# Last 16 units of attention as 8 units of two heads: plain fp32 P times V in two column halves, four products a visit, row sums by VectorE adds

## Chip, cores and metric

The kernel runs on one core of a Trainium2 chip. The metric is the device time of one execution in microseconds (us); lower is better. TensorE (PE, with its weight loads as PEld), VectorE (DVE), ScalarE (ACT), GpSimd (POOL) and SyncE (SP, which issues nearly all DMAs) run side by side, each in the order of its own queue, and wait for one another by semaphores.

## What is computed

Two layers of a diffusion backbone over 256 context and 2048 latent tokens of width 1024. Each layer projects the tokens (3100 columns), runs a bidirectional Mamba-2 scan (SSD), a bidirectional gated DeltaNet scan (GDN) and grouped-query attention (6 query heads, 2 key/value heads, head size 64) on the projections, and adds the gated and projected result to the stream. The part that the change touches:

```python
def block(qi):
    s = jnp.einsum('bqhgd,bkhd->bhgqk', qi, k).astype(jnp.float32) * scale
    pr = jax.nn.softmax(s, axis=-1).astype(v.dtype)
    return jnp.einsum('bhgqk,bkhd->bqhgd', pr, v)
```

Everything is float32, and the scores are large enough that the kernel subtracts each row's maximum before the exponential.

## The kernel before

Tokens stand in 18 tiles of 128 (`NT`). A layer goes through these stages: projections with the weights and tokens split into a high and a low fp32r part (L401, L455); `gating`, `gdn_pre` and `gdn_solve` of the GDN; `ssd_states` and `ssd_out` of the SSD, tile by tile; `gdn_chain`, a serial recurrence of 18 steps with two half-steps each; and the output projection (L1236). Attention is work that is laid beside all of these from the end of the projections on.

An attention unit is one head and 512 queries, 24 units a layer (the first layer has 6 small ones for the context beside them). `unit_max` makes the scores of the unit with queries as rows (`pq`, L536: four products of 512 columns and one of 256 for each of four query tiles), and DVE reduces them to row maxima (`mx`, L538). `unit_main` then goes over the 18 key tiles: two fp32r products give the scores with keys as rows and the maximum subtracted (`pst`, L567 and L568; together called S below), ACT writes exp of it (`pe`, L570), and `pv` (L561) multiplies by V, accumulating in the PSUM tile `po`. V carries a column of ones, so that row 64 of `po` is the row sum. The maxima of the next unit are spread over the key tiles of the present one.

For units 0 to 12 `pv` is one plain fp32 product, 65 columns wide. For units 13 to 23 ACT copies `pe` to fp32r (`ph`, L575), DVE takes the rest (`pl`, L576), V is split in the same way (`vh`, L659), and `pv` is three fp32r products. The exponentials stay in a ring of four tiles.

Order on the engines: the program is written with a priority by place in the text, and a scheduler lays the instructions of each engine in a fixed order. The text emits the first 8 attention units, then `gdn_chain`, then the other 16 units; so the chain goes ahead of units 8 to 23, and these fill what it leaves free. A half-step of the chain has three phases: products of the state on PE (`p<-Sc,kqc`, L1105 and L1114), DVE (`r`, L1109); products on PE (L1119), ACT (`Vc`, L1124); products on PE (L1128, L1130), DVE (new state `Sc`, L1132). `prep` loads the operands of a later step by DMAs on SP (`kqc`, `xf`, `acv`, `er`) into two buffers, and makes `pv` (L1072, L1081) from them.

## Time and profile before

| | us |
|---|---|
| median of 3 runs | 4045.18 (4043.82 to 4050.78) |
| the profiled execution, its own time | 4047.43 |
| its span, first to last instruction | 4045.6 |
| PE busy in it | 3760.3 (93%) |
| DVE busy | 2682.6 (66%) |
| ACT busy | 1831.1 (45%) |
| POOL busy | 1342.1 (33%) |

Busy is the union of an engine's instructions, so a PE instruction counts with the tail in which its last columns drain while the next one already streams. A window row gives the busy time of each engine in a stretch, the granted TensorE clock as a share of 2.4 GHz, and the DMA engines' share.

### The profile page before, as it was taken

Reading aid. Unit: us, or ns where it says so; the run is one execution under the profiler, and the core shown is the slowest. Engines: PE = TensorE matmul, PEld = TensorE weight load, DVE = VectorE, ACT = ScalarE, POOL = GpSimd, SP = SyncE. Lnnn points to the kernel's source line nnn. Section 1 sums busy time; section 2 is a strip of 40 time slices with the busy share of each in tenths; the row PEclk is TensorE's granted clock in tenths of the full one; section 3 lists DMA queues with packets and bytes.
Section 4 is the critical chain, followed back from the end, with each engine's and each line's share of the span. In section 5 each row is a group of like instructions: output and inputs, shape, how many; then the busy total and the mean of one; then the engine's idle time right before and its main releaser. Section 6 shows DMA issues by size and latency. Waiting matters only on the chain. (4 is left out here: it accounts for less than half of the span.)

```text
span 4045.6 us, 69921 instructions
## 1 busy us (share of the span) xinstructions
PE 3760.3 (93%) x25546; PEld 2839.3 (70%) x25546; DVE 2682.6 (66%) x5114; ACT 1831.1 (45%) x3782; POOL 1342.1 (33%) x1710
## 2 busy tenths in 40 slices
PE   8999999888999988887999999999889999889789
PEld 5899999554566655565678999995545566656567
DVE  7556473787778866665547664747886887666633
ACT  5343342443466655662224433424334566556510
POOL 5112130585267422233303130303762573112300
PEclk9999999999999989987999999999999999988889
DMA  6343432353312444547653434322443224444354
GB/s 201 100 141 111 133 110 92 107 156 136 103 55 64 90 108 107 127 100 235 206 168 112 152 104 136 112 99 79 145 135 105 58 66 96 104 103 114 91 173 153
DMA packets 554115, 484.38 MB, mean 120 GB/s; under 512 B 133992, under 2 KB 488620, under 8 KB 553772
## 3 DMA queue, kind: packets, MB, share of 16 engines
q1 hardware_dynamic: 511916, 444.51, 37.7%
q10 hardware_dynamic: 41856, 35.40, 2.9%
q8 instruction: 202, 3.31, 0.3%
q14 instruction: 141, 1.16, 0.1%
HBM read 335.59 MB, written 144.18 MB: 119 GB/s over the span
## 5 line engine op out<-in xcount | busy, mean ns | idle before, releaser
L570 ACT ACTIVATE pe<-pst 128x512 f32<-128x512 f32 (+1 forms) x876 | 512.0, 594 | 635.8 <-PE pst L568 602.2
L538 DVE TENSOR_REDUCE mx<-pq 128x1 f32<-128x512 f32 (+1 forms) x972 | 590.4, 626 | 134.8 <-PE pq L536 130.1
L561 PE MATMUL po<-pe,v 128*65 128x512 f32 x960 | 492.4, 602 | 3.9 <-ACT os__12072 L584 3.9
L536 PE MATMUL pq<-khh,q 128*128 128x512 f32 (+1 forms) x972 | 455.5, 499 | 29.8 <-DVE mx L538 25.9
L567 PE MATMUL pst<-q,khh 128*128 128x512 f32 (+1 forms) x876 | 437.5, 500 | 38.5 <-DVE mx L538 36.4
L455 PE MATMUL ps<-hi,wh 128*128 128x384 f32 (+2 forms) x1296 | 441.1, 340 | 0.0
L455 PE MATMUL ps<-lo,wh 128*128 128x384 f32 (+2 forms) x1296 | 441.1, 340 | 0.0
L455 PE MATMUL ps<-hi,wl 128*128 128x384 f32 (+2 forms) x1296 | 441.0, 340 | 0.0
L576 DVE TENSOR_TENSOR pl<-pe,ph 128x512 fp32r<-128x512 f32 x396 | 318.7, 809 | 108.7 <-ACT ph L575 68.9
L401 PE MATMUL ps<-wh,hi 128*128 128x320 f32 (+1 forms) x1120 | 354.4, 318 | 1.6 <-DVE hi L365 1.6
L568 PE MATMUL pst<-qm,klo 65*128 65x512 f32 (+1 forms) x876 | 355.1, 407 | 0.0
L401 PE MATMUL ps<-wh,lo 128*128 128x320 f32 (+1 forms) x1120 | 349.8, 315 | 1.7 <-DVE lo L366 1.7
L401 PE MATMUL ps<-wl,hi 128*128 128x320 f32 (+1 forms) x1120 | 350.4, 314 | 0.0
L536 PEld LDWEIGHTS pq<-khh,q 128*128 128x128 f32 x972 | 187.3, 195 | 185.0 <-issue 70.2
L376 DVE TENSOR_TENSOR wl<-wt,wh 128x1024 fp32r<-128x1024 f32 (+3 forms) x144 | 175.3, 1246 | 167.2 <-ACT wh L375 165.0
L567 PEld LDWEIGHTS pst<-q,khh 128*128 128x128 f32 x876 | 171.1, 195 | 156.8 <-DVE mx L538 64.1
L575 ACT CAST ph<-pe 128x512 fp32r<-128x512 f32 x396 | 243.5, 619 | 81.9 <-PE po L561 34.9
L561 PE MATMUL po<-ph,vh 128*65 128x512 f32 x792 | 270.1, 423 | 0.1
L455 PEld LDWEIGHTS ps<-lo,wh 128*128 128x128 f32 x1296 | 244.0, 188 | 10.3
L455 PEld LDWEIGHTS ps<-hi,wl 128*128 128x128 f32 x1296 | 243.4, 188 | 10.4
L455 PEld LDWEIGHTS ps<-hi,wh 128*128 128x128 f32 x1296 | 243.4, 188 | 10.2
L1236 PE MATMUL psd<-woh,mh 128*128 128x512 f32 x544 | 217.4, 400 | 16.4 <-ACT mh L1227 15.1
(587 smaller groups left out, 8086.9 us busy)
## 6 DMA issues: line engine op xcount, KB each, us to landing
wt<-in_w_in_dram SPq DMA_DIRECT2D x72, 512.0 KB
wmt<-in_w_mod_dram SPq DMA_DIRECT2D x48, 512.0 KB
pre_d<-pre SPq DMA_DIRECT2D x34, 512.0 KB
acv<-pre_d SPq DMA_DIRECT2D x34, 512.0 KB
kqc<-kt_d SPq DMA_DIRECT2D x68, 256.0 KB
acv<-pre_d SPq DMA_DIRECT2D x68, 256.0 KB
wt<-in_w_in_dram SPq DMA_DIRECT2D x24, 668.0 KB
wt<-in_w_in_dram SPq DMA_DIRECT2D x24, 640.0 KB
```

What stands on the lines that cost most here:

```text
L376: nc.vector.tensor_tensor(out=wl[:, ks, :], in0=wt, in1=wh[:, ks, :].bitcast(F32), op=ALU.subtract)
L401: nc.tensor.matmul(ps, hh[:, k, a], ww[:, k, :], start=(n == 0), stop=(n == 3 * KD - 1))
L455: nc.tensor.matmul(ps, ww[:, k, m * P:(m + 1) * P], hh[:, k, s0:s0 + sn], start=(n == 0), stop=(n == 3 * KD - 1))
L536: nc.tensor.matmul(pq[:, :n], q2[:, u * P:(u + 1) * P], khh[:, kvh, k0t * P + a:k0t * P + a + n], start=True, stop=True)
L538: nc.vector.tensor_reduce(mx[:, u, i:i + 1], pq[:, :n], axis=AX.X, op=ALU.max)
L561: nc.tensor.matmul(po[0:65, :qn], v[:, kt, vs], p[:, :qn], start=(kt == k0t and j == 0), stop=(kt == k1t - 1 and j == len(ops) - 1))
L567: nc.tensor.matmul(pt[:, :qn], khh[:, kvh, ks], q2[:, :qn], start=True, stop=False)
L568: nc.tensor.matmul(pt[:, :qn], klo[:, kvh, ks], qm[:, :qn], start=False, stop=True)
L570: nc.scalar.activation(out=pe[:, :qn], in_=pt[:, :qn], func=AF.Exp, scale=0.125)
L575: nc.scalar.copy(out=ph, in_=pe)
L576: nc.vector.tensor_tensor(out=pl, in0=pe, in1=ph.bitcast(F32), op=ALU.subtract)
L1236: nc.tensor.matmul(ps, a, w[k][:, n * 512:n * 512 + 512], start=(k == 0 and i == 0), stop=(k == KD - 1 and i == 2))
```

## The change

Units 0 to 7 stay as they are (plain fp32). Units 8 to 23 become eight pairs of neighbouring heads on the same queries. `pair_max` runs the two heads' maxima one after the other. `pair_main` makes for each key tile the scores and exponentials of both heads into one tile `pe` of 128 by 2 by 512. P times V is plain fp32, 64 columns of V without the ones: the first head's product writes partitions 0 to 63 of `po`, the second's 64 to 127. It is issued in visits of two key tiles, that is four products in the order head 0, head 1, head 0, head 1. The row sums no longer come from the column of ones: DVE adds the `pe` tiles into `acc` (one add of 128 by 1024 a key tile, 17 a pair), and at the pair's end two products by a matrix of ones sum `acc` over the partitions. The fp32r copies of P and V and their pool go. The ring of `pe` has six pair tiles in place of four single ones, the query rings four buffers in place of three.

```diff
+            def pair_main(h0, q0, qn, k0t, k1t, st):
+                kvh = (h0 // 3, (h0 + 1) // 3)
+                po = ps_o.tile([P, 512], F32, name="po", tag="po")
+                half = (slice(0, 64), slice(64, 128))
+                pend, acc = [], None
+
+                def visit(n, behind_mm):
+                    with tc.high_priority():
+                        for v in range(n):
+                            kt, pe = pend.pop(0)
+                            for j in range(2):
+                                c0 = kvh[j] * 65
+                                mm = nc.tensor.matmul(po[half[j]], v1[:, kt, c0:c0 + 64], pe[:, j], start=(kt == k0t), stop=(kt == k1t - 1))
+                                if v == 0 and j == 0:
+                                    behind(mm, behind_mm)
+
+                for kt in range(k0t, k1t):
+                    ks = slice(kt * P, (kt + 1) * P)
+                    pe = ap_.tile([P, 2, 512], F32, name="pe", bufs=PB)
+                    for j in range(2):
+                        pt = aslot("pst")
+                        nc.tensor.matmul(pt, khh[:, kvh[j], ks], st["q2"][j], start=True, stop=False)
+                        mm = nc.tensor.matmul(pt, klo[:, kvh[j], ks], st["qm"][j], start=False, stop=True)
+                        nc.scalar.activation(out=pe[:, j], in_=pt, func=AF.Exp, scale=0.125)
+                        if j == 0:
+                            yield
...
+                        nc.vector.tensor_tensor(out=acc, in0=acc, in1=pe, op=ALU.add)
+                    pend.append((kt, pe))
+                    if len(pend) == 3:
+                        visit(2, mm)
+                    yield
+                visit(len(pend), mm)
...
+                for j in range(2):
+                    nc.tensor.matmul(pl[half[j]], cc("ones")[:, 0:64], acc[:, j], start=True, stop=True)
...
-                    if kt in sp:
-                        ph = spl.tile([P, 512], F32R, name="ph", bufs=2)
-                        pl = spl.tile([P, 512], F32R, name="pl", bufs=2)
-                        nc.scalar.copy(out=ph, in_=pe)
-                        nc.vector.tensor_tensor(out=pl, in0=pe, in1=ph.bitcast(F32), op=ALU.subtract)
```

The order of the instructions moves in three places that matter below. Line numbers of the changed program are its own (two more up to the attention, 51 more in the chain).

First, SP at the end of the projections of the first layer. L526 and L527 load the queries of the first units; the others are projection weights (`wt`) and stores of its results. Before:

```order
L374 DMA wt<-in_w_in_dram 128x4x256
L188 DMA qkw<-in_q_norm_w_dram 128x64
L188 DMA qkw<-in_k_norm_w_dram 128x64
L335 DMA qt_d<-qo 128x128 x3
L526 DMA q_10914<-qt_d 128x512
L526 DMA q_10992<-qt_d 128x256
L526 DMA q_11026<-qt_d 128x512
L527 DMA qm<-qt_d 64x512
L527 DMA qm<-qt_d 64x256
L527 DMA qm<-qt_d 64x512
L488 DMA cv_d<-th 128x769
L374 DMA wt<-in_w_in_dram 128x4x256 x2
```

and in the changed program:

```order
L376 DMA wt<-in_w_in_dram 128x4x334 x2
L465 DMA zt_d<-z 128x384 x2
L411 DMA zn_d<-zn 128x334
L465 DMA zt_d<-z 128x384
L411 DMA zn_d<-zn 128x334 x5
L424 DMA zn_d<-zn 128x306 x5
L526 DMA q_10911<-qt_d 128x512
L526 DMA q_10989<-qt_d 128x256
L526 DMA q_11023<-qt_d 128x512
L526 DMA q_11207<-qt_d 128x256
L527 DMA qm<-qt_d 64x512
```

The loads moved from the middle of the last token group, with most of its weights still to be loaded, to behind nearly all its stores. On PE the 20 products of the first unit's maxima, which stood among the projection's, stand behind its last one. The second layer moves in the same way.

Second, DVE in `ssd_out`, about one token tile in its middle (`m`, `t`, `sq` are the SSD's, `mx` the attention's). Before:

```order
L844 TENSOR_TENSOR m_9978<-m_9978,pd 128x384
L862 TENSOR_TENSOR t_9893<-py,t_9893 128x384
L845 TENSOR_TENSOR m_9978<-m_9978,ee 128x384
L850 TENSOR_TENSOR t_9986<-po_10010,ecum 128x192
L850 TENSOR_TENSOR t_9987<-po_10010,ecum 128x192
L821 SCALAR_TENSOR_TENSOR m_10071<-cst,sp,m_10071 128x128 x6
L866 TENSOR_SCALAR sq<-sq 128x1
L850 TENSOR_TENSOR t_9986<-po_10035,ecum 128x192
L850 TENSOR_TENSOR t_9987<-po_10035,ecum 128x192
L868 TENSOR_SCALAR t_9893<-t_9893,sq 128x384
```

and in the changed program:

```order
L624 TENSOR_TENSOR acc<-acc,pe 128x1024
L538 TENSOR_REDUCE mx<-pq 128x1 x2
L913 TENSOR_TENSOR t_9890<-py,t_9890 128x384
L872 SCALAR_TENSOR_TENSOR m_10068<-cst,sp,m_10068 128x128 x6
L895 TENSOR_TENSOR m_9975<-m_9975,pd 128x384
L624 TENSOR_TENSOR acc<-acc,pe 128x1024
L896 TENSOR_TENSOR m_9975<-m_9975,ee 128x384
L917 TENSOR_SCALAR sq<-sq 128x1
L901 TENSOR_TENSOR t_9983<-po_10007,ecum 128x192
L901 TENSOR_TENSOR t_9984<-po_10007,ecum 128x192
L538 TENSOR_REDUCE mx<-pq 128x1 x2
```

Two to three adds stand in each tile, among the SSD's own instructions. From the first instruction of `ssd_out` to the chain's first, DVE has 105 `mx`, 39 `pl` and no add in the first layer before, and 111, none and 49 after; in the second layer 94, 31 and none, and 97, none and 43.

Third, PE in the middle of the chain of the first layer, from one half-step's first products (L1105, now L1156) to its last (L1128, now L1179). Before:

```order
L1105 MATMUL p<-Sc,kqc 64x64 x8
L1114 MATMUL p<-Sc,kqc 64x64 x2
L536 MATMUL pq<-khh,q_18401 128x256
L567 MATMUL pst<-q_18102,khh 128x512
L568 MATMUL pst<-qm,klo 128x512
L536 MATMUL pq<-khh,q_18401 128x512
L561 MATMUL po<-ph,vh_16904 65x512
L561 MATMUL po<-ph,vh_16905 65x512
L561 MATMUL po<-pl,vh_16904 65x512
L1119 MATMUL p<-r,xf_12683 64x64 x2
```

and in the changed program, with the phase that follows:

```order
L1156 MATMUL p<-Sc,kqc 64x64 x8
L1165 MATMUL p<-Sc,kqc 64x64 x2
L536 MATMUL pq<-khh,q_17927 128x512 x2
L613 MATMUL pst<-q_17702,khh 128x512
L614 MATMUL pst<-qm,klo 128x512
L1170 MATMUL p<-r,xf_12752 64x64 x2
...
L536 MATMUL pq<-khh,q_17927 128x256
L613 MATMUL pst<-q_17702,khh 128x512
L614 MATMUL pst<-qm,klo 128x512
L604 MATMUL po<-pe,v_352 64x512 x4
L536 MATMUL pq<-khh,q_17927 128x512 x2
```

The three P times V products between two phases are gone; a visit of four stands in about every third gap. In the whole chain PE has 158 S, 155 `pq` and 481 fp32r `pv` products in the first layer before, and 164, 137 and 42 visits after (second layer 167, 160 and 505; 169, 143 and 43). DVE has 159 `pl` before and 74 adds after (167 and 77). The last attention product stood two half-steps before the chain's end and stands four before it.

## Rows read from the trace of the kernel before

**Rows 1.** The page's first part: busy us, share of the span, instructions.

```profile
PE 3760.3 (93%) x25546; PEld 2839.3 (70%) x25546; DVE 2682.6 (66%) x5114; ACT 1831.1 (45%) x3782; POOL 1342.1 (33%) x1710
```

**Rows 2.** Windows of `ssd_out` and the chain, first and second layer.

```profile
core 0: us, PE busy (x) PEld busy (x) DVE busy (x) ACT busy (x) POOL busy (x), PEclk, DMA share, GB/s
1117.00:1393.00 276.00, 265.67 (x1251) 171.38 (x1249) 229.60 (x457) 189.79 (x492) 174.41 (x185) 1.00 0.25 66
1393.00:1836.00 443.00, 379.58 (x4994) 258.84 (x4994) 284.64 (x485) 256.78 (x494) 114.19 (x96) 0.89 0.50 116
3157.00:3393.00 236.00, 225.29 (x985) 144.22 (x984) 192.72 (x383) 150.97 (x395) 148.25 (x160) 0.97 0.22 59
3393.00:3836.00 443.00, 390.79 (x4986) 266.41 (x4984) 295.16 (x500) 267.76 (x515) 106.87 (x92) 0.91 0.47 107
```

**Rows 3.** Windows of `ssd_out` with plain units, then with split ones (columns as above).

```profile
1100.00:1296.00 196.00, 191.80 (x832) 120.05 (x830) 155.16 (x322) 124.56 (x339) 124.46 (x131) 1.00 0.20 59
1296.00:1392.00 96.00, 90.54 (x476) 60.33 (x475) 89.50 (x166) 71.31 (x166) 50.09 (x56) 0.99 0.31 72
...
3318.00:3380.00 62.00, 57.06 (x256) 38.23 (x255) 55.33 (x105) 40.80 (x99) 34.84 (x40) 0.94 0.19 49
```

**Rows 4.** Waits in the first layer's chain: who, for whom, us, times, longest.

```profile
POOL sd L1107 <- DVE Sc L1132: 187.6, 31, 8.6
...
DVE kqc L1061 <- DMA kqc<-kt_d: 42.0, 15, 4.2
...
DVE pl L576 <- ACT ph L575: 31.4, 43, 2.6
PEld pv L1072 <- issue: 24.7, 15, 4.3
...
DVE pl L576 <- PE po L561: 15.3, 18, 2.7
```

**Rows 5.** Timeline, PE around one tile of `ssd_states`: start, length, instructions.

```profile
1014.95 1.02 PE L561 MATMUL po<-pe,v 128*65 128x512 f32 x2
...
1015.90 0.87 PE L794 MATMUL pst<-xd,bn 128*64 128x192 f32 x8
1016.70 0.42 PEld L781 LDWEIGHTS pt<-cst,xb 128*128 128x128 f32 x4 [0.28 <-issue]
```

**Rows 6.** Timeline, PE in the chain: two fp32r products of P times V.

```profile
1608.09 0.63 PE L561 MATMUL po<-ph,vh 128*65 128x512 f32 x2
```

**Rows 7.** Groups by line and form: count, busy us, mean ns, idle before.

```profile
L576 DVE TENSOR_TENSOR pl<-pe,ph 128x512 fp32r<-128x512 f32 x396 | 318.7, 809 | 108.7 <-ACT ph L575 68.9 <-PE po L561 27.4 <-ACT vt L1076 5.0
L376 DVE TENSOR_TENSOR wl<-wt,wh 128x1024 fp32r<-128x1024 f32 x72 | 88.3, 1251 | 77.8 <-ACT wh L375 75.6 <-DMA q<-qt_d 2.2
L575 ACT CAST ph<-pe 128x512 fp32r<-128x512 f32 x396 | 243.5, 619 | 81.9 <-PE po L561 34.9 <-DVE pl L576 26.5 <-issue 2.8
```

**Rows 8.** Instructions of L576 in the chain: ns least, median, most.

```profile
L576 DVE TENSOR_TENSOR pl<-pe,ph x161: 673/692/1753, 1391.5 to 1812.9; 128x512 fp32r<-128x512 f32 x161
```

**Rows 9.** Groups of DVE in the first layer's `ssd_out`.

```profile
L538 DVE TENSOR_REDUCE mx<-pq 128x1 f32<-128x512 f32 x83 | 55.5, 678 | 14.8 <-PE pq L536 14.5
...
L576 DVE TENSOR_TENSOR pl<-pe,ph 128x512 fp32r<-128x512 f32 x38 | 32.7, 868 | 3.2 <-ACT ph L575 3.1
```

**Rows 10.** All maxima, from the page's fifth part.

```profile
L538 DVE TENSOR_REDUCE mx<-pq 128x1 f32<-128x512 f32 (+1 forms) x972 | 590.4, 626 | 134.8 <-PE pq L536 130.1
```

**Rows 11.** Timeline, the chain's last two states in the first layer.

```profile
1818.92 0.42 DVE L1132 TENSOR_TENSOR Sc<-sd,p 128x256 f32<-128x256 f32 x1
...
1825.24 0.36 DVE L1132 TENSOR_TENSOR Sc<-sd,p 128x256 f32<-128x256 f32 x1
```

**Rows 12.** The attention's start: a window behind the projections, and the split of V.

```profile
711.00:740.00 29.00, 25.21 (x91) 13.46 (x92) 25.51 (x49) 13.07 (x33) 4.96 (x8) 1.00 0.21 65
...
L659 DVE TENSOR_TENSOR vh<-v,vh 128x2322 fp32r<-128x2322 f32 x1 | 2.6, 2567 | 0.0
```

**Rows 13.** Groups of PE from 540 to 715 us: the first maxima among the projections.

```profile
L536 PE MATMUL pq<-khh,q 128*128 128x512 f32 (+1 forms) x24 | 8.6, 374 | 0.9 <-ACT pe L570 0.5 <-DVE mx L538 0.3
```

More of the change, by code (lines that the diff above doesn't have):

```diff
@@ L35 @@
 GT = 768
+PB = 6
+NS = 8
 def rev(t):
@@ L587, in unit_main, with pair_max @@
                 nc.sync.dma_start(mx_d[640 + h * 64:704 + h * 64, q0:q0 + qn], os_[ob:ob + 64, :qn])
+                yield
+            def pair_max(h0, q0, qn, k0t, k1t, st):
+                st.update(q2=[], qm=[])
+                gens = []
+                for j in range(2):
+                    sj = {}
+                    g = unit_max(h0 + j, q0, qn, k0t, k1t, sj)
+                    for i, _ in enumerate(g):
+                        if i == 0:
+                            st["q2"].append(sj["q2"])
+                            st["qm"].append(sj["qm"])
+                        yield
@@ new lines, in pair_main @@
+            def pair_main(h0, q0, qn, k0t, k1t, st):
[6 more added lines that the diff above has]
+                        for v in range(n):
+                            kt, pe = pend.pop(0)
+                            for j in range(2):
[12 more added lines that the diff above has]
+                        if j == 0:
+                            yield
+                    if kt == k0t:
+                        pass
+                    elif kt == k0t + 1:
+                        acc = ap_.tile([P, 2, 512], F32, name="acc", bufs=1)
+                        nc.vector.tensor_tensor(out=acc, in0=pend[0][1], in1=pe, op=ALU.add)
+                    else:
+                        nc.vector.tensor_tensor(out=acc, in0=acc, in1=pe, op=ALU.add)
+                    pend.append((kt, pe))
+                    if len(pend) == 3:
+                        visit(2, mm)
+                    yield
+                visit(len(pend), mm)
+                os_ = ap_.tile([P, 512], F32, name="os2", bufs=1)
+                nc.scalar.copy(out=os_, in_=po)
+                pl = aslot("pl")
+                for j in range(2):
+                    nc.tensor.matmul(pl[half[j]], cc("ones")[:, 0:64], acc[:, j], start=True, stop=True)
+                sm_ = ap_.tile([65, 512], F32, name="sm_", bufs=1)
+                nc.scalar.copy(out=sm_, in_=pl[0:65])
+                for j in range(2):
+                    nc.sync.dma_start(sm_d[None, HQ * q0 + (h0 + j) * qn:HQ * q0 + (h0 + j + 1) * qn], sm_[64 * j:64 * j + 1])
+                nc.sync.dma_start(mx_d[640 + h0 * 64:768 + h0 * 64, q0:q0 + qn], os_)
@@ L630, in attention @@
                 small = [] if last else [(h, 0, LC, 0, TC) for h in range(HQ)]
-                sb, ss_ = [{} for _ in big], [{} for _ in small]
-                mb = [unit_max(*un, st) for un, st in zip(big, sb)]
+                units = [(1, un) for un in big[:NS]] + [(2, un) for un in big[NS::2]]
+                sb, ss_ = [{} for _ in units], [{} for _ in small]
+                mb = [(unit_max if n == 1 else pair_max)(*un, st) for (n, un), st in zip(units, sb)]
                 ms = [unit_max(*un, st) for un, st in zip(small, ss_)]
@@ L653, in attention @@
                         pass
-                for i, un in enumerate(big):
-                    if i == 13:
-                        for _ in range(2):
-                            vh.append(spl.tile([P, NT, 129], F32R, name=f"vh{len(vh)}", bufs=1))
-                        nc.scalar.copy(out=vh[0], in_=v1)
-                        nc.vector.tensor_tensor(out=vh[1], in0=v1, in1=vh[0].bitcast(F32), op=ALU.subtract)
-                    spn = () if i < 13 else range(NT)
+                at = 0
+                for i, (n, un) in enumerate(units):
                     nxt = ms[i:i + 1] + mb[i + 1:i + 2]
-                    left = (21 + 3) * (i + 1 < len(big)) + 3 * (i < len(small))
+                    left = (24 * units[i + 1][0] if i + 1 < len(units) else 0) + 6 * (i < len(small))
+                    steps = n * (NT - 4)
                     done = 0
-                    for j, _ in enumerate(unit_main(*un, sb[i], spn)):
-                        want = left * (j + 1) // (NT - 4)
+                    for j, _ in enumerate((unit_main if n == 1 else pair_main)(*un, sb[i])):
+                        want = left * (j + 1) // steps
                         adv(nxt, want - done)
@@ L671, in attention @@
                             pass
-                    if i >= 14:
-                        next(side_work, None)
-                    if i % HQ == HQ - 1:
-                        if small and i == HQ - 1:
+                    at += n
+                    for k in range(at - n, at):
+                        if k >= 14:
+                            next(side_work, None)
+                    if at % HQ == 0:
+                        if small and at == HQ:
                             inv(0, LC)
-                        inv(big[i][1], 512)
+                        inv(un[1], 512)
                     yield
```

21 lines of the change are left out of this document (6 added, 15 removed).

## Prediction

> **What bounds the kernel now.** I read the page's first part, then windows stage by stage, then waits and single instructions in the stages that the change touches. Over the whole span PE is busy 93% and DVE 66% [rows 1], which would say that only PE's work counts. The windows say more [rows 2]: `ssd_out` takes 276 and 236 us with PE at 96 and 95%, the chain 443 us in both layers with PE at 86 and 88%, DVE at 64 and 67%, ACT at 58 and 60%, and a granted clock of 0.89 and 0.91.
>
> Inside `ssd_out` the bound depends on the attention beside it [rows 3]. With plain units PE is busy 191.80 of 196 us (98%) and DVE 79%; with split units DVE is busy 89.50 of 96 us (93%) and PE 94%; in the second layer's split stretch they are at 89 and 92%. So split units, which give DVE a subtraction a key tile, already bring it to the point where it limits. The chain is no engine's alone: 36 half-steps in 443 us are 12.3 us each, while the last two states, with no attention between them, stand 6.3 us apart [rows 11]. Attention roughly doubles a half-step. Waits there [rows 4]: GpSimd waits 187.6 us for the state, which is the recurrence; DVE 42.0 us for the load of `kqc`; and DVE 31.4 us for `ph` and 15.3 us for `po` ahead of `pl`, both waits that come from the split.
>
> **PE.** A plain product of 65x512 is two passes that together take 1.02 us [rows 5], and two fp32r products take 0.63 us [rows 6]. Both hold a tail that the next instruction overlaps. With a pass of 0.23 us for fp32r the tail is 0.63 − 2 × 0.23 = 0.17, three split products cost 0.69, and a plain one costs 1.02 − 0.17 = 0.85, or 0.43 a pass. The trace has no plain 512-column product on a half of the columns, but eight records of 192 columns on two halves: 0.87 us [rows 5]. A pass of 192 columns is 0.43 × 192/512 = 0.16 us; four overlapped steps and the tail make 0.81, eight in turn 1.45. So the halves run together. The changes of form cost something: from the plain product's start to L794's are 0.95 us instead of 0.85, and from there to the next line's 0.80 instead of 0.64. I allow 0.3 us a visit for both. A visit is then 4 × 0.43 + 0.3 = 2.0 us for four products, where four split products cost 2.76 and four plain ones 3.4. The bounds are 1.7 (no cost of the change) and 3.7 (no overlap).
>
> **DVE.** Out go the subtractions, 0.69 us at the median in the chain [rows 8] and 0.868 in `ssd_out` [rows 9]. In come adds of 128x1024, not in the trace. The nearest row is L376, 128x1024 with two inputs, 1.251 us [rows 7]. `pl` was 0.176 us longer beside the busy GpSimd of `ssd_out` than in the chain. One such wait an instruction would make an add 1.43 us there, and in proportion to its length it would be 1.25 × 0.868/0.692 = 1.57. I take 1.4, bounds 1.25 and 1.57. In the chain I take 1.25.
>
> The Trainium skill ("SBUF — State Buffer", section "SBUF: two separate sides") says that GpSimd and a VectorE operation with two SBUF inputs take a shared port as an exclusive lock for a whole instruction. The longer `pl` beside a busy GpSimd agrees. By the rule an add waits once as `pl` does (1.43 us), and it speaks against this change too, since longer instructions keep GpSimd out for longer; the sum by it would be 2 to 3 us higher.
>
> **`ssd_out`.** Between the same instructions the first layer gets 6 more maxima at 0.626 us [rows 10], 49 adds, and loses 39 `pl`: DVE 229.6 + 3.8 + 49 × 1.4 − 39 × 0.868 = 268.1 us. The second layer gets 3 maxima, 43 adds, and loses 31: 192.7 + 1.9 + 60.2 − 26.9 = 227.9. DVE alone then nearly fills the old length. At the 93% of the split stretch the stages become 288.3 and 245.0 us: **+21 us** in sum. PE doesn't contradict this, it has room at 94%. Bounds: at 97% busy and adds of 1.25 us, 269 and 228 us (−15); at 89% and 1.57 us, 311 and 264 us (+63). GpSimd, at 174 of 276 us, would at worst wait out the 35 us that the two-input work grows by (68.6 − 33.9), and stays at 76%.
>
> **Chain.** PE in the first layer: 481 products × 0.23 = 111 us go, 42 visits × 2.0 and 4 us of row sums come; 18 fewer `pq` save 4 and 6 more S of two products cost 3: −24 us. The second: 116 against 90, −4, +1: −29. DVE: 159 × 0.69 go, 74 × 1.25 come, 18 maxima go: −29, second layer −31. ACT loses 159 and 167 copies of 0.619 us [rows 7]: −98 and −103. No engine gets more. PE's −24 at a share of 86% is 28 us. The two more half-steps without attention at the end, at 6.3 us instead of 12.3, I count at little, since what stood there is done in fuller half-steps before. The 46.7 us in which DVE waited ahead of `pl` lose their cause, though how much of them ended a half-step can't be seen. Against that, the loads of `prep` pace a part (42.0 us of waits for `kqc`), and a visit of 2.0 us in one piece can stand ahead of a phase's products where three products of 0.23 us stood. I take −30 a layer, **−60 us**. Bounds: 0, if loads and the recurrence set the pace, and −75 a layer (28 + 46.7), if those waits all count.
>
> **Start of attention.** The first unit's maxima leave the projections: 20 × 0.23 = 4.6 us of PE less in a stage that PE bounds ([rows 13]: 24 instructions at 8.6 us with their tails). They now stand behind it and go at DVE's pace, 20 × 0.63 = 12.6 us, in a stretch that was nearly full, PE 25.21 and DVE 25.51 of 29 us [rows 12]. `vh`, 2.6 us of DVE, goes. Between −4.6, if gating covers all, and 12.6 − 2.6 = +10, if PE idles for all of it, I take +4 a layer, nearer the full price since both engines were nearly full: **+8 us**, bounds −9 and +20. The attention that this delays is in the counts of the later stages already.
>
> What I cost at nothing: row-sum products, 1.1 us eight times a layer, in the counts above for the chain and otherwise beside a DVE that limits; the larger ring of exponentials; ACT, which no window here shows over 75% busy.
>
> **Sum** against the profiled execution, 4047.4, which stands 2.2 us above the median of the runs: 4047.4 + 21 − 60 + 8 = 4016 us.
>
> **Rivals.**
>
> 1. DVE loses more in `ssd_out`, and the kernel ends slower. An add stands 1.4 us in DVE's queue ahead of the SSD's own instructions (`m`, `t`, `sq`), on which PE, GpSimd and ACT wait in turn; a `pl` stood 0.87. For it: two to three adds stand in each token tile, and 89 to 93% was reached with the shorter instruction. Against: two thirds of DVE's instructions there are no part of a tile's own sequence and can fill. With DVE at 85% the stages are 315 and 268 us, +71 and 4047 + 71 − 60 + 8 = 4066 us. It decides from a loss of 60 us, at 86.5% busy. Chance 0.20.
>
> 2. The chain is paced by its loads and waits, and gains nothing: 4076 us. For it: the DVE's wait for `kqc`, PE's share of only 86%, and half-steps of the same 443 us in both layers though PE's busy time differs by 11 us [rows 2]. Against: 6.3 us a half-step where no attention stands between. Chance 0.17.
>
> 3. The stalls of the split go with it, and the chain gains 75 us a layer: 3926 us. For it: DVE, ACT and PE all get less work, and nothing but attention makes a half-step 12 us. Against: the phases still wait in the order of the queues. Chance 0.13.
>
> 4. The halves don't run together with 512 columns, so that the change doesn't do what it says: 4 × 0.43 = 1.7 us more a visit, 85 visits in both chains, +145 us and some of the others on top: 4190 us. Against it stands the row of L794. Chance 0.04.
>
> The forecast keeps 0.46.
>
> **How the numbers follow.** No change can be told within 0.2%, 8 us: 4037 to 4053. The forecast's own range, 3975 to 4055, takes the terms' bounds at about half their reach; 0.38 of its chance lies below 4037 and 0.08 within. Rival 3 is faster throughout; rivals 1 and 2 spread 40 us around their times and give 0.05 to no change and 0.03 to faster; the rest and rival 4 are slower. Faster 0.54, same 0.13, slower 0.33. From 3940 to 4085 the range leaves out rival 4, most of rival 3 and the upper third of the first two, some 2 in 10.
>
> **What the profile after would show.** Products of a visit: the two halves' starts some ns apart, a visit of 2.0 us (1.7 to 3.7). Adds: a mean of 1.4 us in `ssd_out`, 1.25 in the chain. `ssd_out`: 288 and 245 us with DVE at 93% and PE well under 95%; PE at 96% again would show that DVE doesn't bound. The chain: about 413 us, half-steps of 11.4 us, DVE's wait for `kqc` still there; 443 us with that wait grown speaks for rival 2. Behind the projections: an idle PE of some us among the first maxima. A stage outside these that differs by more than 5 us (projections, `gdn_pre`, `gdn_solve`, output projection), or a lower clock in the chain because PE idles more, would make the sum wrong.

## The result and the profile after

The changed kernel takes 4214.91 us (median of 4 runs, 4193.2 to 4221.08) against 4047.98 us: a ratio of 1.0404, with an interval of 1.0364 to 1.0443. It is 4% slower, outside the range of 3940 to 4085 us and on the other side of the forecast 4016. Every ratio here and below is to runs of the kernel before that were made beside it (medians of 4033.70 to 4040.22 us for the experiments), so ratios can be compared with one another, and times only roughly.

The first two parts of its page, busy time of each engine and the granted clock of TensorE in 40 slices (9 is full), beside [rows 1]:

```profile
PE 3843.6 (91%) x25214; PEld 2769.7 (66%) x25214; DVE 2743.5 (65%) x4988; ACT 1601.7 (38%) x3384; POOL 1365.5 (32%) x1710
...
PEclk8999998999989977787999999999999788788889
```

PE's share of the span falls from 93 to 91% though its busy time grows by 83 us, and the mean granted clock falls from 0.959 to 0.913. DVE's busy time grows by 61 us of 4200 and stays at 65%: no engine's busy time shows where 171 us went. The windows do. `ssd_out` and the chain, first layer and second; `ssd_out` is taken from PE's first `py` product (L861, now L912) to its first product of the state (L1105, now L1156), and the chain from there to the last phase:

```profile
core 0: us, PE busy (x) PEld busy (x) DVE busy (x) ACT busy (x) POOL busy (x), PEclk, DMA share, GB/s
...
1138.00:1459.00 321.00, 285.88 (x1213) 166.01 (x1213) 263.90 (x452) 159.74 (x429) 183.49 (x181) 0.86 0.22 57
1459.00:1941.00 482.00, 407.98 (x4880) 234.52 (x4879) 278.50 (x391) 175.64 (x349) 127.62 (x101) 0.80 0.49 116
...
3266.00:3557.00 291.00, 263.94 (x1045) 153.91 (x1045) 227.09 (x399) 140.88 (x376) 154.70 (x157) 0.82 0.21 56
3557.00:4006.00 449.00, 390.98 (x4765) 225.02 (x4769) 263.59 (x384) 166.49 (x339) 105.44 (x91) 0.83 0.45 104
```

and the kernel before, cut in the same way:

```profile
1127.00:1396.00 269.00, 257.74 (x1215) 166.38 (x1214) 222.89 (x439) 180.61 (x465) 168.64 (x179) 0.99 0.27 69
1396.00:1824.00 428.00, 373.54 (x4972) 256.28 (x4974) 279.18 (x477) 252.69 (x488) 109.75 (x93) 0.90 0.48 112
...
3162.00:3400.00 238.00, 226.71 (x1052) 145.89 (x1051) 193.68 (x382) 153.41 (x399) 145.71 (x157) 0.97 0.25 64
3400.00:3832.00 432.00, 384.09 (x4902) 262.16 (x4903) 287.49 (x484) 261.41 (x504) 104.14 (x89) 0.91 0.46 106
```

So `ssd_out` grew by 52 and 53 us, the chain by 54 and 17, and the stretch ahead of `ssd_out`, in which the first pairs run, by 17 and 13; all other stages together gave 35 us back, 17 of them between the first layer's chain and the end of its output projection (267 us for 284). In `ssd_out` the clock went from 0.99 and 0.97 to 0.86 and 0.82, and PE is idle for 35 and 27 us, where it was idle for 11 in each. No engine is full: DVE is busy 82 and 78% (83 and 81% before), PE 89 and 91%. PE's waits for maxima in the first `ssd_out`, before and after (us, times, longest):

```profile
PE pst L567 <- DVE mx L538: 2.6, 5, 0.7
PE pq L536 <- DVE mx L538: 2.1, 6, 0.5
```
```profile
PE pq L536 <- DVE mx L538: 6.8, 9, 1.8
PE pst L613 <- DVE mx L538: 6.1, 6, 1.9
```

What PE did before its clock fell is seen at one place. Timeline of PE and DVE in `ssd_out`:

```profile
start us, us, engine line op out<-in xcount [idle before <-releaser]
...
1251.75 2.88 DVE L872 SCALAR_TENSOR_TENSOR m<-cst,sp,m 128x128 f32<-128x128 f32 x4
1251.97 0.59 PE L891 MATMUL pd<-rr,sufr 128*128 128x384 f32 x2 [1.10 <-DVE t L901]
...
1253.60 0.39 PE L614 MATMUL pst<-qm,klo 65*128 65x512 f32 x1
1254.56 1.01 DVE L538 TENSOR_REDUCE mx<-pq 128x1 f32<-128x512 f32 x2
1255.29 1.22 PE L536 MATMUL pq<-khh,q 128*128 128x512 f32 x2 [1.30 <-DVE mx L538]
```

and the windows around it:

```profile
1240.80:1247.60 6.80, 6.80 (x31) 3.95 (x28) 3.62 (x7) 1.37 (x4) 1.00 (x1) 0.72 0.07 19
1247.60:1254.90 7.30, 5.28 (x25) 3.59 (x24) 6.20 (x10) 4.95 (x16) 6.60 (x7) 1.00 0.19 54
1254.90:1261.70 6.80, 6.41 (x14) 2.98 (x16) 6.80 (x12) 1.58 (x4) 1.71 (x2) 0.50 0.17 48
1261.70:1268.50 6.80, 6.21 (x35) 4.31 (x31) 6.54 (x12) 2.68 (x6) 3.99 (x5) 1.00 0.02 4
```

PE waits twice for DVE, 1.10 us for `t` and 1.30 us for a maximum that stands in DVE's queue behind four instructions of the SSD. It is busy 5.28 of 7.30 us; then the granted clock is 0.50 for 6.8 us, and in that stretch PE gets through 14 instructions instead of 25 to 35. By an estimate, half of the 6.41 us in which PE was busy at half clock, the two waits of together 2.4 us cost some 3.2 us more. DVE is busy for all of the slow stretch. The place is not an exception: 76 stretches at half clock begin in this trace, and ahead of 75 of them, over a time as long as the second row, PE had idled for more than its 9% of the whole span (30% at the median).

For the whole kernel this can be added up from the page and the mean clock: PE's idle time is the span less its busy time, and the loss by the clock is taken as (1 − mean clock) × span, as if PE were busy in all of it.

| | ratio to before | span, us | PE busy, us | clock | idle, us | loss by clock, us | the rest, us |
|---|---|---|---|---|---|---|---|
| before | 1 | 4045.6 | 3760.3 | 0.959 | 285 | 166 | 3594 |
| after | 1.0404 | 4216.8 | 3843.6 | 0.913 | 373 | 367 | 3477 |
| no_adds | 1.0054 | 4078.1 | 3785.4 | 0.927 | 293 | 298 | 3488 |
| every_2nd | 1.0246 | 4135.2 | 3786.5 | 0.926 | 349 | 306 | 3481 |
| dup | 1.0426 | 4221.3 | 3900.6 | 0.935 | 321 | 274 | 3626 |
| no_adds_dup | 1.0258 | 4127.5 | 3847.2 | 0.948 | 280 | 215 | 3633 |
| nohp | 1.0416 | 4203.7 | 3926.8 | 0.956 | 277 | 185 | 3742 |
| same_half | 1.0728 | 4342.5 | 4038.9 | 0.930 | 304 | 304 | 3735 |
| ns24 | 1.0025 | 4038.5 | 3803.6 | 0.972 | 235 | 113 | 3691 |
| single64 | 1.0381 | 4190.2 | 4022.5 | 0.971 | 168 | 122 | 3901 |

The rest is, by this estimate, PE's work at full clock. The change cut it by 117 us, and got 88 us of idle time and 201 us of clock for it. The other rows belong to the experiments below.

### The profile page after: what moved, and what is told of

It reads as the page before. It is cut to its first block, busy times and chain, and to the rows that moved or that the text cites. A ratio compares the mean times of both kernels' runs of the same rounds, so it can differ in the third digit from the quotient of the medians.

```text
span 4216.8 us, 68181 instructions
## 1 busy us (share of the span) xinstructions
PE 3843.6 (91%) x25214; PEld 2769.7 (66%) x25214; DVE 2743.5 (65%) x4988; ACT 1601.7 (38%) x3384; POOL 1365.5 (32%) x1710
## 5 line engine op out<-in xcount | busy, mean ns | idle before, releaser
L615 ACT ACTIVATE pe<-pst 128x512 f32<-128x512 f32 x576 | 335.0, 595 | 577.7 <-PE pst L614 572.9
L624 DVE TENSOR_TENSOR acc<-acc,pe 128x1024 f32<-128x1024 f32 x256 | 349.6, 1366 | 94.1 <-ACT pe L615 92.3
L604 PE MATMUL po<-pe,v 128*64 128x512 f32 x1152 | 364.2, 732 | 0.0
L613 PE MATMUL pst<-q,khh 128*128 128x512 f32 x576 | 291.9, 507 | 26.4 <-DVE mx L538 14.6
L558 PE MATMUL po<-pe,v 128*65 128x512 f32 x600 | 304.4, 598 | 1.4 <-ACT os__11633 L574 0.9
L378 DVE TENSOR_TENSOR wl<-wt,wh 128x1024 fp32r<-128x1024 f32 (+3 forms) x144 | 175.2, 1247 | 176.0 <-ACT wh L377 175.9
L566 ACT ACTIVATE pe<-pst 128x512 f32<-128x512 f32 x300 | 172.8, 589 | 294.0 <-PE pst L564 292.3
L614 PE MATMUL pst<-qm,klo 65*128 65x512 f32 x576 | 255.5, 444 | 0.0
L1287 PE MATMUL psd<-woh,ml 128*128 128x512 f32 x544 | 215.9, 397 | 0.3
```

The source lines that it names most:

```text
L378: nc.vector.tensor_tensor(out=wl[:, ks, :], in0=wt, in1=wh[:, ks, :].bitcast(F32), op=ALU.subtract)
L558: nc.tensor.matmul(po[0:65, :qn], v1[:, kt, kvh * 64:kvh * 64 + 65], pe[:, :qn], start=(kt == k0t), stop=(kt == k1t - 1))
L604: mm = nc.tensor.matmul(po[half[j]], v1[:, kt, c0:c0 + 64], pe[:, j], start=(kt == k0t), stop=(kt == k1t - 1))
L613: nc.tensor.matmul(pt, khh[:, kvh[j], ks], st["q2"][j], start=True, stop=False)
L614: mm = nc.tensor.matmul(pt, klo[:, kvh[j], ks], st["qm"][j], start=False, stop=True)
L615: nc.scalar.activation(out=pe[:, j], in_=pt, func=AF.Exp, scale=0.125)
```

## Experiments

Theory A, formed from this: the adds hold up DVE, PE idles in short gaps, and the gaps halve its clock. Rivals: B, products on a column half bring the clock down by themselves; C, the order makes PE wait (visits of four products ahead of others, loads); D, PE's work sets the time.

**no_adds.** The adds go, and the row sums are made from a constant tile.

```diff
+            one_ = ap_.tile([P, 2, 512], F32, name="one_", bufs=1)
...
-                    if kt == k0t:
-                        pass
-                    elif kt == k0t + 1:
-                        acc = ap_.tile([P, 2, 512], F32, name="acc", bufs=1)
-                        nc.vector.tensor_tensor(out=acc, in0=pend[0][1], in1=pe, op=ALU.add)
-                    else:
-                        nc.vector.tensor_tensor(out=acc, in0=acc, in1=pe, op=ALU.add)
+                    acc = one_
```

> The changed kernel with the adds of the exponentials left out (the row sums are taken from a constant tile, so 136 VectorE adds a layer go and nothing else). Theory A, the adds hold up VectorE, TensorE then idles ahead of the maxima and its clock falls: the two ssd_out stages come back from 321 and 291 us to 265 to 280 and 235 to 250, TensorE's idle time there from 35 us to under 15, the clock there to 0.95 or more, and the time is 4040 to 4100 us. Theory B, the column halves themselves bring the clock down: it stays at 0.82 to 0.88 in both stages and the time stays above 4170. Theory C, the order (visits, loads) makes TensorE wait: the stages stay within 15 us of 321 and 291 and the time above 4150.

4051.34 us, 1.0054 (1.0031 to 1.0077). The adds cost 3.5% of the time, about 140 us. The profiled execution was the slowest of seven, 4079.9. Its windows:

```profile
1120.00:1432.00 312.00, 291.23 (x1222) 171.32 (x1222) 193.75 (x404) 159.75 (x429) 159.86 (x178) 0.86 0.23 60
1432.00:1865.00 433.00, 382.54 (x4878) 221.40 (x4878) 177.85 (x314) 173.82 (x351) 118.84 (x100) 0.85 0.53 126
3176.00:3433.00 257.00, 241.12 (x1085) 143.30 (x1083) 174.78 (x353) 142.69 (x382) 140.65 (x159) 0.91 0.23 63
3433.00:3867.00 434.00, 393.09 (x4757) 230.85 (x4755) 163.55 (x304) 164.74 (x338) 96.72 (x89) 0.83 0.45 106
```

The total is as theory A had it, its places only partly: the chain comes back to 433 and 434 us and the second `ssd_out` to 257, but the first stays at 312 at a clock of 0.86, with DVE busy 62%. So gaps and a low clock come without the adds too. GpSimd changes as well: in `ssd_out` it is busy 183.49 and 154.70 us with the adds and 159.86 and 140.65 without, for about as many instructions. How much of the price comes by way of this longer GpSimd, no run here separates.

**every_2nd.** Every second add is left out.

```diff
-                        nc.vector.tensor_tensor(out=acc, in0=pend[0][1], in1=pe, op=ALU.add)
-                    else:
+                        nc.vector.tensor_tensor(out=acc, in0=one_, in1=pe, op=ALU.add)
+                    elif kt % 2 == 0:
```

> Every second add left out (9 of 17 a pair stay; the row sums are wrong by it, and nothing else is left out). If the price follows VectorE's time: 1.020 to 1.028 of before, halfway. If one add in a row is hidden and only two close together delay the maxima and the chain: 1.003 to 1.015.

4137.64 us, 1.0246 (1.0225 to 1.0266): about halfway between 1.0404 and 1.0054, as the number of adds would have it. Its windows:

```profile
1130.00:1426.00 296.00, 270.35 (x1188) 161.98 (x1189) 224.57 (x421) 157.69 (x425) 173.61 (x180) 0.88 0.24 62
1426.00:1903.00 477.00, 403.82 (x4912) 228.82 (x4913) 234.44 (x363) 178.13 (x355) 123.70 (x101) 0.83 0.53 125
3218.00:3486.00 268.00, 242.28 (x1051) 143.93 (x1051) 199.32 (x374) 139.03 (x375) 150.82 (x159) 0.88 0.23 61
3486.00:3934.00 448.00, 383.65 (x4749) 221.96 (x4751) 221.86 (x352) 166.03 (x340) 106.07 (x93) 0.85 0.47 112
```

Stage by stage it is not halfway. Both `ssd_out` get back about half of their loss (296 and 268 us), but the chains, 477 and 448, stay within 5 us of the changed kernel's: there half of the adds cost as much as all, with DVE busy 49%. The first `ssd_out` is even shorter than the 312 us of no_adds, whose profile is of its slowest execution; a single stage of one profile is worth no more than that.

**half_adds** and **adds_late.** Each add as two of 128x512; or each add written with its visit, one to two key tiles later.

```diff
...
-                        nc.vector.tensor_tensor(out=acc, in0=acc, in1=pe, op=ALU.add)
+                    for j in range(2):
+                        if kt > k0t:
+                            a0 = (pend[0][1] if kt == k0t + 1 else acc)[:, j]
+                            nc.vector.tensor_tensor(out=acc[:, j], in0=a0, in1=pe[:, j], op=ALU.add)
```
```diff
                     if len(pend) == 3:
+                        add(pend[:2])
                         visit(2, mm)
...
```

> The changed kernel with each add of 128x1024 made as two of 128x512, the first behind the first head's exponential. The same elements; some 0.1 us more of VectorE a key tile for the second instruction. If the length in the queue is what delays the maxima (A1): TensorE's idle time in the ssd_out stages falls from 35 and 27 us by a third or more, time 4120 to 4170. If VectorE's total does it (A2): idle time and stages as before or longer, 4190 to 4240.

> The same adds, each written one to two key tiles later, with its visit, so that VectorE doesn't stand in an add's wait for an exponential while the chain's or the maxima's work is behind it. If these waits (40.7 us in the first layer's chain) are what the adds cost in the chain: its length goes from 482 and 449 us to 440 to 455, and the time to 4130 to 4180. If the adds' own time does it: 4195 to 4240.

4232.75 us, 1.0475 (1.0456 to 1.0494), and 4223.24 us, 1.0471 (1.0454 to 1.0489). Both are a little slower than the changed kernel. So the length of an add is not the price: with halves the first `ssd_out` has 45 us of PE idle instead of 35. The wait of the adds for the exponential is not answered, because the edit didn't take it away. DVE's wait in the first layer's chain, in the changed kernel and in adds_late:

```profile
DVE acc L624 <- ACT pe L615: 40.7, 38, 3.1
```
```profile
DVE acc L614 <- ACT pe L623: 40.6, 38, 3.2
```

**gp_adds.** The adds on GpSimd.

```diff
-                        nc.vector.tensor_tensor(out=acc, in0=acc, in1=pe, op=ALU.add)
+                        nc.gpsimd.tensor_tensor(out=acc, in0=acc, in1=pe, op=ALU.add)
```

> The changed kernel with the adds on GpSimd (L869 makes 128x768 there in about 1.5 us, so 2 to 2.5 us an add). In ssd_out GpSimd goes from 183 of 321 us to over 280 and takes VectorE's place as the engine that is late: the stages stay at 300 or more and 265 or more. In the chain it has room, and the stage goes from 482 and 449 us to near the 433 and 434 without adds. Time 4100 to 4180. If the adds hurt only as work of VectorE in any stage: as without adds, 4050 to 4080.

4268.48 us, 1.0565 (1.0534 to 1.0596), slower than the 4100 to 4180 expected. Its group of GpSimd:

```profile
L624 POOL TENSOR_TENSOR acc<-acc,pe 128x1024 f32<-128x1024 f32 x256 | 615.0, 2402 | 156.1 <-ACT pe L615 144.3 <-DVE tm L853 6.9 <-DVE mx L538 2.0
```

`ssd_out` grows to 367 and 312 us with GpSimd busy for 284 and 248 of them; it makes operands of the SSD (`m`, `rr`, `t`), and these now stand in its queue among adds of 2.4 us. The chain, 459 and 452 us, comes only half of the way back in the first layer and not in the second.

**single64.** 24 single units with 64 columns of V, after **ns24**, 24 single units with 65.

```diff
-NS = 8
+NS = 24
...
-                    nc.tensor.matmul(po[0:65, :qn], v1[:, kt, kvh * 64:kvh * 64 + 65], pe[:, :qn], start=(kt == k0t), stop=(kt == k1t - 1))
+                    nc.tensor.matmul(po[0:64, :qn], v1[:, kt, kvh * 65:kvh * 65 + 64], pe[:, :qn], start=(kt == k0t), stop=(kt == k1t - 1))
```

> The changed kernel with 24 plain single units and no pair: no split copies, no adds, every product of P and V plain at 0.85 us. By price, 198 products a layer cost 0.16 us more than the split ones, some 30 us a layer if TensorE bounds, less where it had idled: 4050 to 4110 us. TensorE is the busier engine everywhere, so by theory A its clock in the chain is above the 0.90 and 0.91 of the kernel before. Theory B gives the same.

> The 24 plain single units with 64 columns of V in place of 65 (the row sums are left out and a constant is stored for them): each product stands on one column half, alone, and lasts as long as before. Theory A: the clock stays at 0.96 or more, and only the change of form costs, 0.1 to 0.3 us beside each of 432 products a layer where TensorE bounds: 4080 to 4220. Theory B, column halves bring the clock down: half-clock time in the two chains goes from 48 and 34 us to over 100 each, and the mean clock to 0.94 or less.

ns24: 4041.61 us, 1.0025 (1.0012 to 1.0039), below the 4050 to 4110 expected, at a clock of 0.972. single64: 4190.83 us, 1.0381 (1.0355 to 1.0406), at 0.971. `ssd_out` and the chains of single64:

```profile
1087.00:1362.00 275.00, 271.95 (x1147) 146.67 (x1147) 185.54 (x389) 154.88 (x417) 163.05 (x179) 1.00 0.25 64
1362.00:1841.00 479.00, 445.11 (x4849) 215.90 (x4849) 180.39 (x341) 164.95 (x334) 107.12 (x93) 0.93 0.44 99
3205.00:3452.00 247.00, 245.35 (x1011) 131.39 (x1009) 165.41 (x347) 137.11 (x367) 142.47 (x159) 1.00 0.25 65
3452.00:3903.00 451.00, 427.90 (x4741) 206.30 (x4740) 176.79 (x335) 163.20 (x330) 100.40 (x89) 0.97 0.43 101
```

A product on a column half doesn't bring the clock down: theory B falls for a half alone (for two halves together see no_adds_visit1 below). What it costs is put down to the change of form, from full width to a half and back: 0.0356 × 4040 us over 864 products (24 units, 18 key tiles, two layers) is 0.17 us a product. PE's work in the table grows by more, 210 us or 0.24 a product, and 67 us of idle time go. This agrees with the Trainium skill ("TensorEngine Tiling (Array Packing)", section "Key Properties"), by which a change of the tiling mode makes TensorE drain.

**same_half.** Both heads' products on the first half, so that none run together.

```diff
-                                mm = nc.tensor.matmul(po[half[j]], v1[:, kt, c0:c0 + 64], pe[:, j], start=(kt == k0t), stop=(kt == k1t - 1))
+                                mm = nc.tensor.matmul(po[half[0]], v1[:, kt, c0:c0 + 64], pe[:, j], start=(kt == k0t and j == 0), stop=(kt == k1t - 1 and j == 1))
...
```

> The changed kernel with both heads' products written to the first column half, so that no two run together (the two heads are mixed in the output; all else as in the changed kernel). By price a visit goes from 1.9 to 3.6 us, 72 visits a layer, +245 us: 4400 to 4460. Theory A: TensorE is busy where it idled, the clock in ssd_out and the chain rises from 0.80 to 0.86 to over 0.90, and gives back a good part: 4250 to 4350. Theory B, a product on half of the columns lowers the clock: it falls below 0.80 in both, and the time is above 4450.

4328.2 us, 1.0728 (1.0696 to 1.076). By the table PE's work grows by 258 us over the changed kernel, where the price said 245; the time grows by some 130, and idle time and clock give 69 and 63 us back. This work, which lengthens the visits, is paid about half, most of it in the chains: they take 536 and 510 us.

**dup** and **no_adds_dup.** The first score product is made twice, with the adds and without.

```diff
+                        nc.tensor.matmul(pt, khh[:, kvh[j], ks], st["q2"][j], start=True, stop=True)
                         nc.tensor.matmul(pt, khh[:, kvh[j], ks], st["q2"][j], start=True, stop=False)
```

> The changed kernel with the first of the two score products of each key tile and head of a pair made twice (the second overwrites the first): 288 more products of 0.23 us a layer on TensorE, 66 us a layer at full clock, nothing else. Theory A in its sharper form (TensorE has idle gaps that it can't use, they halve its clock for 3 to 17 us each, and the missing work of P times V is what had filled them before): the extra work fills gaps, half-clock time falls from 735 us to under 600, and the time is 4180 to 4270. Rival D, TensorE's work sets the time as it stands: +132 us at full clock and more at the half, 4340 to 4400.

> No adds (row sums left out) and the doubled score product. Without adds the kernel took 1.0054 of before, with half-clock time of 130 and 149 us in the chains. If idle gaps and the clock set the chain (A), 132 us more of TensorE's work leave the time where it is or lower it: 4030 to 4080, half-clock time in the chains under 90 us each. If the adds had been what left room for the doubled product (D: TensorE sets the time as soon as VectorE doesn't): 4130 to 4190.

dup: 4214.6 us, 1.0426 (1.0398 to 1.0454). 576 more products in two layers, 132 us at 0.23, and the time moves by 0.2%, with intervals that overlap. The two chains:

```profile
1458.00:1914.00 456.00, 409.23 (x5065) 248.02 (x5066) 266.64 (x393) 172.45 (x345) 114.07 (x93) 0.91 0.46 103
3556.00:4004.00 448.00, 405.61 (x4932) 243.59 (x4928) 267.86 (x387) 170.50 (x341) 111.53 (x89) 0.92 0.44 102
```

Their clock is 0.91 and 0.92 in place of 0.80 and 0.83. The first is 26 us shorter with more work in it, but what follows it in the layer, up to the end of the output projection, is 23 us longer (290 for 267), so the layer gains nothing to speak of. These products, placed with the scores, are free in the changed kernel. Without the adds they are not: no_adds_dup takes 4137.0 us, 1.0258 (1.0236 to 1.028), 0.020 or 82 us more than no_adds. That is in the range of rival D (4130 to 4190), where theory A had expected 4030 to 4080. So A in its sharp form, that extra work of PE is free wherever the clock is low, falls: same_half paid about half of it, this run 82 of 132 us.

**ns14.** 14 single units and 5 pairs, so that `ssd_out` has none.

```diff
-NS = 8
+NS = 14
```

> The changed kernel with 14 plain single units and 5 pairs, so that ssd_out has plain units alone and the pairs stand in the chain. Theory A (adds in ssd_out cost it): ssd_out 265 to 285 and 235 to 255 us with TensorE's clock at 0.97 or more, the chain as in the changed kernel with some 480 and 450 us at a clock of 0.80 to 0.84; time 4080 to 4130. If everything lost is lost in ssd_out: 4020 to 4060. Theory B (halves bring the clock down): as theory A in ssd_out, and the chain at 0.80 whatever else it does.

4077.4 us, 1.0106 (1.0089 to 1.0124). `ssd_out` is back at 270 and 231 us; the chain takes 451 and 450 us (some 480 and 450 were expected) at a clock of 0.84 and 0.85, against 428 and 432 at 0.90 and 0.91 before. So the pairs cost in both stages, and about three quarters of the loss goes with the three pairs that stand beside the SSD.

**visit1** and **no_adds_visit1.** Visits of one key tile; **ns14_visit1**, the same with 14 single units; **nohp**, visits without their priority and without the order behind the scores.

```diff
-                    if len(pend) == 3:
-                        visit(2, mm)
+                    if len(pend) == 2:
+                        visit(1, mm)
```
```diff
-                    with tc.high_priority():
+                    if True:
...
-                                if v == 0 and j == 0:
-                                    behind(mm, behind_mm)
```

> Visits of one key tile, two products instead of four. A change of form costs 0.17 us by the single 64-column products, and there are 72 more visits a layer: +25 us if TensorE sets the time. If a block of 1.9 us ahead of the chain's phases (C) is what lengthens the chain, it falls by 10 us or more a layer and the time to 4170 to 4200; otherwise 4215 to 4250.

> No adds (row sums left out) and visits of one key tile. If the adds (1.0054 of before without them, 1.0404 with) and the size of a visit (1.0326 with two products) are separate prices, both gone: 0.99 to 0.998 of before, half-clock time under 480 us. If smaller visits only help VectorE's adds: 1.003 to 1.009, and half-clock time near the 594 us of the kernel without adds.

> 14 plain single units, then 5 pairs with visits of one key tile, nothing left out. With 14 units the kernel took 1.0106 of before, and 5 of the 8 pairs' share of the gain by smaller visits would be 0.005: 1.002 to 1.008, with half-clock time of 100 to 120 us in each chain in place of 140 and 137. Below 0.998 it would beat the kernel before.

> Visits without their raised priority and without the order behind the scores, so that the scheduler places each product as it does all others. If the raised priority (C) makes TensorE wait: idle time in ssd_out and the chain falls by 20 us or more a layer, time 4100 to 4180. If the adds and the thinner work of TensorE do it: 4200 to 4260, since visits are broken up and change form more often.

visit1 takes 4166.86 us, 1.0326 (1.0298 to 1.0354): 0.8% faster than the changed kernel, although it changes form more often. So the block of four products has a share, as C had it. no_adds_visit1 takes 4050.32 us, 1.0035 (1.0016 to 1.0054), which is no clear gain over 1.0054. Its `ssd_out`, first layer and second:

```profile
1125.00:1385.00 260.00, 248.13 (x1185) 143.61 (x1186) 189.53 (x394) 156.81 (x424) 162.16 (x178) 0.98 0.28 72
...
3162.00:3397.00 235.00, 224.75 (x1060) 129.41 (x1060) 169.77 (x351) 138.53 (x375) 144.47 (x159) 0.99 0.26 70
```

Both halves run together in most of these visits (two products in 1.08 us), at a clock of 0.98 and 0.99, so theory B falls for them too. The stage is as short as before the change, but the first chain takes 464 us, and with it the time stays. The clock of its executions is 0.948 at the median against 0.934 of no_adds, for about the same time: a higher clock alone doesn't make a faster kernel here. ns14_visit1 takes 4097.16 us, 1.0139 (1.0121 to 1.0156), slower than ns14 and than its forecast: smaller visits shorten the whole only in the full change. nohp takes 4200.63 us, 1.0416 (1.04 to 1.0431). Its `ssd_out`:

```profile
1153.00:1470.00 317.00, 304.23 (x1239) 156.53 (x1241) 267.86 (x459) 160.31 (x430) 180.75 (x179) 1.00 0.22 58
...
3285.00:3561.00 276.00, 264.75 (x1097) 138.33 (x1097) 238.04 (x406) 140.84 (x378) 161.53 (x160) 0.99 0.22 58
```

Visits are torn apart here, most into single products; PE's work is 265 us more than in the changed kernel, its clock in `ssd_out` is 1.00 and 0.99 and it is busy 96%, and the stage takes 317 and 276 us where the changed kernel takes 321 and 291 at 0.86 and 0.82. The same time, once spent in work and once in gaps and at half clock.

## Why the prediction was wrong

**The counts and the prices of single instructions were right.** A visit, timeline of PE at full and at half clock:

```profile
1106.04 1.94 PE L604 MATMUL po<-pe,v 128*64 128x512 f32 x8
...
1156.16 3.49 PE L604 MATMUL po<-pe,v 128*64 128x512 f32 x8
```

Eight passes in 1.94 us with the tail; the halves run together (2.0 was forecast), and rival 4 falls. The adds in `ssd_out` and in the chain, groups of DVE:

```profile
L624 DVE TENSOR_TENSOR acc<-acc,pe 128x1024 f32<-128x1024 f32 x44 | 63.2, 1437 | 4.5 <-ACT pe L615 4.3
```
```profile
L624 DVE TENSOR_TENSOR acc<-acc,pe 128x1024 f32<-128x1024 f32 x75 | 101.7, 1355 | 41.2 <-ACT pe L615 40.7
```

1.44 us for 1.4 and 1.36 for 1.25. DVE's busy time in `ssd_out` was forecast at 268.1 and 227.9 us and is 263.9 and 227.1.

**The first step that failed** is "at the 93% of the split stretch the stages become 288.3 and 245.0 us". DVE stands at 82 and 78%, and the stages at 321 and 291: +105 us in place of +21, beyond the bound of +63. The share of 93% was read in a stretch where PE was busy 94% at a clock of 0.99 [rows 3]; it was no property of DVE. The runs show PE idle for 35 and 27 us instead of 11 in each, more of it in waits for DVE, and the stages get shorter with the adds: half of them give 296 and 268 us, none 312 and 257. The reading is that with products at the new price PE has less to do between two results of DVE, so that a wait for one becomes a gap. The step "PE doesn't contradict this, it has room at 94%" took room for something that helps. Here the idle time went with a mean clock of 0.86 and 0.82, at half for 6.8 us at the place shown. The Trainium skill ("TensorE: Matmul & The Clock Gate", section "HAM oscillation — how this bites in real kernels") tells of a kernel whose TensorE idles between bursts and is throttled again at each; the rows at 1247 to 1262 us show it here, after gaps of 1.10 and 1.30 us, shorter than that kernel's waits.

**The second** is "PE's −24 at a share of 86% is 28 us", from which came −60 us in the chain. It gave +54 and +17. The chain's products are PE's too, and at a clock of 0.80 and 0.83 instead of 0.90 and 0.91 everything on PE is slower, attention and recurrence: PE's busy time there didn't fall by 24 and 29 us but grew by 34 and 7. Waits in the first layer's chain, before (with 42.0 us of DVE for `kqc` [rows 4]) and after:

```profile
DVE r L1109 <- PE p L1105: 9.6, 16, 1.1
DVE Sc L1132 <- PE p L1130: 13.2, 16, 2.0
PE pv L1072 <- DMA acv<-pre_d: 12.8, 7, 3.9
```
```profile
DVE r L1160 <- PE p L1156: 41.1, 20, 4.7
DVE Sc L1183 <- PE p L1181: 29.2, 17, 5.0
DVE kqc L1112 <- DMA kqc<-kt_d: 12.6, 8, 3.3
PE pv L1123 <- DMA acv<-pre_d: 39.6, 13, 7.1
```

The recurrence now waits for PE: DVE's waits for the chain's own products grow from 22.8 to 70.3 us. The 46.7 us ahead of `pl` did go, but 40.7 us of the adds' waits for the exponential stand in their place. Rival 2 had the direction of the chain, no gain, but not its sign: DVE's wait for `kqc`, which was to grow, fell to 12.6 us, while PE's wait for the load of `acv` grew. The first chain gets shorter when DVE's work goes (no_adds, 433 us), when PE gets more (dup, 456) and with smaller visits (visit1, 451): it doesn't have one bound.

**The third** is what stood at nothing. The stretch ahead of `ssd_out`, in which the first pairs run, is in no term of the sum and took 30 us more in two layers. Most of the 35 us that other stages gave back are in none either; so the terms that were missed nearly balance, and the error of the sum is that of `ssd_out` and the chain.

**The start** was priced at +8 us and cost nothing: PE is idle there as foretold, 20.83 of 29 us busy at a clock of 0.59 where it was 25.21 at 1.00 [rows 12], but from the projections' end to the first product of `ssd_states` it takes 299 and 302 us where it took 302 and 306.

**Rival 1** had the direction and the place, "DVE loses more in `ssd_out`", and two thirds of the price there, +71 of +105 us; its time of 4066 us still counted on −60 in the chain. What it lacked is the clock, which stood only as a last caution ("a lower clock in the chain because PE idles more"). Its reason, an add of 1.4 us ahead of the SSD's own instructions, isn't borne out as such: adds of half the length are no better. The argument that kept its chance low, "two thirds of DVE's instructions there are no part of a tile's own sequence", reads the counts the wrong way round: of the 439 DVE instructions of the first `ssd_out` before, 105 are `mx` and 39 `pl`, a third. (A slip without effect: DVE's −31 us in the second layer's chain comes to −30 by the prediction's own prices.)

What is shown: the adds cost 3.5 of the 4.0%, and more on GpSimd; to leave out half of them gives back about half of that, in `ssd_out` and hardly in the chains; the column halves don't lower the clock; with the adds in place, doubled score products cost nothing that the intervals can tell and longer visits about half of their work. What is argued only: that the adds do this by the gaps that they leave on PE, and that a kernel with the same gaps and a clock held at full would be faster. No run here holds one of the two and moves the other. Open is whether the adds' wait for the exponential matters in the chain, since adds_late left it as it was, and why, without the adds, 106 us less work of PE (3488 against 3594 in the table) still give 0.5% more time. The profile names maxima in front of PE, but no run here separates them.

## What to carry to other kernels

Before an engine is relieved, look at what it does with the time: where it waits in turn for results of another, less work on TensorE can come back as gaps, and here gaps went with half clock. Forecast such a stage from PE's idle time and clock, not from its busy share alone. Work that is put on the engine that PE waits for isn't free because that engine is busy only 80%: the 272 adds, 374 us of DVE, cost about 140 us. And try the plain form first: 24 plain single units (ns24, 1.0025) are within 0.4% of the kernel with split ones, so the split that the change replaced had brought little.

## What the runs showed of the hardware

- After two gaps of 1.10 and 1.30 us the granted clock was 0.50 (1.2 of 2.4 GHz) for 6.8 us, in which PE was busy 6.41 us: by an estimate some 3.2 us lost behind 2.4 us of gaps, at this place of the changed kernel.
- A plain product on a column half among full-width ones costs 0.17 us more than the same product at 65 columns (single64 against ns24: 864 products, 144 us), with nothing beside it on the other half.
- Four plain products of 512 columns, two on each column half, took 1.94 us together at full clock; the two halves ran side by side.
- An add of 128x1024 took 2.40 us on GpSimd (gp_adds) and 1.36 to 1.44 us on VectorE (the changed kernel).
